# The upper part of the gated one-hot in a tile of its own, with a token's 128 elements side by side

## The chip, the cores and the metric

One core of a Trainium2 chip runs the whole program. The metric is the device time of one execution, in microseconds (us); lower is better.

## The reference

The program is a two-layer encoder trunk over 256 tokens of width 1024. Each layer is a mixer (SSD in layer 0, retention in layer 1), a PEER expert layer and a gated per-layer input; a final RMSNorm closes it. The change lies in the PEER layer alone, whose core is this:

```python
idx = jnp.take_along_axis(cand_idx, top_pos, axis=-1)   # i1 * 128 + i2, 8 heads x 16 picks a token
gate = jax.nn.softmax(top_s, axis=-1)
...
hid = jax.nn.gelu(jnp.einsum('tkd,td->tk', u[ib], xb), approximate=False)
return jnp.einsum('tk,tkd->td', (gb * hid).astype(xb.dtype), v[ib])
```

Each token picks 128 of 128 x 128 = 16384 experts (`i1` and `i2` each run over 128), takes `gelu(u . x)` for each, weights it with its gate and sums the rows of `v`.

## The kernel before

No expert is gathered. The kernel computes the inner products of all 16384 experts with all 256 tokens, and multiplies them with a gate matrix that is zero where an expert was not picked. `H` (128 partitions x 128 x 256, FP32) holds the products: partition and middle index are the two halves of the expert's number, the last index is the token.

**The loop over u** (lines 1224 to 1241) has 128 iterations a layer. An iteration loads 512 KB of `peer_u`, turns it on VectorE (L511), splits it into a rounded half `wh` on ScalarE (L516) and a rest `wl` on GpSimd (L519), and multiplies both with the normed tokens in 24 matmuls of 256 columns (L1237, L1238, L1241) into one PSUM bank `m` (two of them in turn). The next iteration takes the GELU of the bank: ScalarE writes `H` where no gate stands yet (L1201), or writes back to PSUM (L1204), and VectorE multiplies that into the gates that stand already (L1205).

**The first half of the iterations** also works off the selection (top-16, index arithmetic, softmax) on VectorE. When it is done, the second half builds the gate matrix: 64 blocks of 4 tokens, one block started in each iteration. A block passes through four iterations, one step in each, and `g_slot` issues the steps in the order mm, hot, apply, lo, each for another block:

- `g_hot`: VectorE compares an iota with the indices `i1` and `i2` of 4 tokens, which gives two one-hot planes in the FP16 tile `oh` (128 partitions x 2 x 128 x 4; the partitions are the 128 picks, the last index is the token; L1169). A second VectorE instruction multiplies the first plane with the FP16 upper part of the gates, in place (L1171). The iota and the gates (`gt`) lie in PSUM.
- `g_lo`: ScalarE multiplies the gated plane of each token with the ratio of the gate's lower to its upper part and writes it to `ol` (L1177, four instructions of 128 elements).
- `g_mm`: TensorE multiplies, for each token, the transposed second plane with the gated plane (upper part) and then with `ol` (lower part), both into the same 128 columns of a PSUM bank `g` (L1183, 8 matmuls and 8 weight loads a block). The weights `oh[:, 1, :, j]` and the moving operand `oh[:, 0, :, j]` are read with a step of 4 elements (8 bytes), `ol[:, j]` with a step of 1.
- `g_apply`: ScalarE writes the gates to `H` where the product is still to come (L1193), VectorE multiplies them into the products that stand already (L1195).

`oh` has two buffers, so `g_hot` of block b+2 waits for `g_mm` of block b, which stands just ahead of it in the same iteration. `ol` has one buffer, the PSUM banks `g` two. Behind the loop comes the sum over `v` (L1266, 12 matmuls of 512 columns for each of 128 tiles), which the change does not touch.

`diag` (L262) makes a small tile `dg` for the RMSNorms; `spread` reads it soon after. The instructions of every engine are issued in the order in which the code is written; no planner moves them.

Of the kernel before, what the change touches and what calls it, by code (L numbers as in the profile page):

```python
# [8 lines left out]
F32 = mybir.dt.float32  # L9
F32R = mybir.dt.float32r  # L10
F16 = mybir.dt.float16
I32 = mybir.dt.int32
U32 = mybir.dt.uint32
AF = mybir.ActivationFunctionType
# [4 lines left out]
P = 128  # L19
# [68 lines left out]
def trunk(ctx: ExitStack, tc: tile.TileContext, a, out, dbg=None, stop=None):  # L88
    nc = tc.nc
    pe, act, dve, pool, sp = nc.tensor, nc.scalar, nc.vector, nc.gpsimd, nc.sync  # L90
# [5 lines left out]
    small = ctx.enter_context(tc.tile_pool(name="small", bufs=2))  # L96
# [142 lines left out]
    class Sums:  # L239
# [19 lines left out]

        def diag(self, n, src=None):  # L260
            v = self.root(n, src)
            dg = small.tile([P, 2, P], F32, name="dg", tag="sq", bufs=4)  # L262
            for tb in range(2):
                dve.tensor_scalar(dg[:, tb], ident, v[:, tb:tb + 1], None, op0=OP.mult)
            return dg
# [169 lines left out]
    G1 = const.tile([P, T], F32, name="G1")  # L435
# [15 lines left out]
    ps = acc.tile([P, 512], F32, name="ps")  # L451
# [494 lines left out]
    def peer(l, st):  # L946
# [210 lines left out]
        gt = bank[2][:, :128].bitcast(F16)  # L1157
# [7 lines left out]
        def g_hot(b):  # L1165

            oh = small.tile([P, 2, P, 4], F16, name="oh", bufs=2)
            t = slice(4 * b, 4 * b + 4)
            dve.tensor_tensor(oh, i4.unsqueeze(1).to_broadcast([P, 2, P, 4]),  # L1169
                              G3[:, 0:2, t].unsqueeze(2).to_broadcast([P, 2, P, 4]), op=OP.is_equal)  # L1170
            dve.tensor_mul(oh[:, 0], oh[:, 0], gt[:, t].unsqueeze(1).to_broadcast([P, P, 4]))  # L1171
            return oh, small.tile([P, 4, P], F16, name="ol", bufs=1)

        def g_lo(b, oh, ol):
            for j in range(4):
                t = 4 * b + j
                act.activation(ol[:, j], oh[:, 0, :, j], AF.Copy, scale=G1[:, t:t + 1])  # L1177

        def g_mm(oh, ol):
            ps = gps.tile([P, 512], F32, name="g")  # L1180
            for j in range(4):
                for i in range(2):
                    pe.matmul(ps[:, j * P:(j + 1) * P], oh[:, 1, :, j], ol[:, j] if i else oh[:, 0, :, j],  # L1183
                              start=j == 0 and i == 0, stop=i == 1, skip_group_check=True)
            return ps

# [20 lines left out]
        def g_slot(i, times=lambda: None):  # L1207

            ap, mm, lo, b = gst["ap"], gst["mm"], gst["lo"], gst["next"]
            gst.update(ap=None, mm=lo, lo=None)  # L1210
            if mm:
                gst["ap"] = mm[0], g_mm(*mm[1])
            if b < T // 4 and not bg:
                gst["lo"] = b, g_hot(b)
                gst["next"] += 1
            if ap:
                g_apply(*ap, i)
            if lo:
                g_lo(lo[0], *lo[1])
            times()  # L1220
            return ap or mm or lo
# [236 lines left out]
```

## Time and profile before

| | |
|---|---|
| median of 3 runs | 2245.3 us (2243.55 to 2249.71) |
| profiled execution | 2246.1 us, its span 2244.2 us |
| TensorE (PE) busy | 2165.3 us, 96% of the span |
| weight loads (PEld) | 2006.2 us, 89% |
| VectorE (DVE) | 1563.2 us, 70% |
| ScalarE (ACT) | 1210.4 us, 54% |
| GpSimd (POOL) | 878.4 us, 39% |
| blocks of the gate matrix | 128 (64 a layer), first `g_hot` at 521.1 us, last at 1833.8 us |

The span runs from the first to the last instruction; the 1.9 us beside it are the launch. Busy times of PE come from matmuls whose ends are modelled, and a matmul's duration overlaps the next one's; what a matmul costs in a dense stretch is read from the distance of two starts. PE's weight loads run beside its matmuls. In rows, L1183 names the line, `g<-oh` is a matmul of the upper part and `g<-ol,oh` one of the lower part.

### The profile page before, as it was taken

What the parts mean: (1) busy time and instruction counts of PE and PEld (TensorE: products, weight loads), DVE (VectorE), ACT (ScalarE), POOL (GpSimd) and SP (SyncE); (2) the same over time, 40 slices, a digit from 0 to 9 for tenths busy, and PEclk for the clock granted to TensorE, in tenths of its full rate; (3) what the DMA queues carried; (4) which work ended last, traced back from release to release, by engine and by line L of the source; (5) the groups of instructions that cost most, each with busy time, mean ns of one, the idle gap of its engine ahead of it and who ended that gap; (6) DMA issues with size and microseconds to landing.
All of it is one profiled execution on the core that took longest, in us unless ns stands there. A gap on an engine that the chain in (4) does not pass through costs nothing. (4 is left out here: it accounts for less than half of the span.)

```text
span 2244.2 us, 39809 instructions
## 1 busy us (share of the span) xinstructions
PE 2165.3 (96%) x15013; PEld 2006.2 (89%) x15013; DVE 1563.2 (70%) x2625; ACT 1210.4 (54%) x2063; POOL 878.4 (39%) x408
## 2 busy tenths in 40 slices
PE   7899899999999999999989999999999999999997
PEld 7788899999999888888888999999999998888886
DVE  7478678887788655555587366889678875555556
ACT  4544444546888644444553444445588874444444
POOL 5743248886666200000044123788766640000002
PEclk9999999999999999999999999999999999999998
DMA  5432467756555555555645455776555545666653
GB/s 165 136 106 86 143 192 181 183 139 160 143 148 144 160 195 190 196 193 192 201 160 174 138 166 177 176 191 154 160 148 145 145 147 194 193 194 192 194 192 104
DMA packets 219577, 370.27 MB, mean 165 GB/s; under 512 B 24240, under 2 KB 163192, under 8 KB 219384
## 3 DMA queue, kind: packets, MB, share of 16 engines
q1 hardware_dynamic: 219064, 367.19, 55.0%
q8 instruction: 118, 1.93, 0.4%
q14 instruction: 75, 0.61, 0.1%
q10 hardware_dynamic: 320, 0.53, 0.1%
HBM read 364.48 MB, written 1.05 MB: 163 GB/s over the span
## 5 line engine op out<-in xcount | busy, mean ns | idle before, releaser
L135 ACT CAST wh<-raw 128x1024 fp32r<-128x1024 f32 x429 | 450.3, 1052 | 519.7 <-PE ps L1266 362.5
L138 DVE TENSOR_TENSOR wl<-raw,wh 128x1024 fp32r<-128x1024 f32 x365 | 453.6, 1246 | 393.9 <-ACT wh L135 393.9
L519 POOL TENSOR_TENSOR wl<-raw,wh 128x1024 fp32r<-128x1024 f32 x256 | 615.5, 2406 | 240.5 <-ACT wh L516 231.1
L1266 PE MATMUL ps<-wh,X 128*128 128x512 f32 x2048 | 509.2, 390 | 4.6 <-ACT X L186 4.6
L1237 PE MATMUL m<-X,wh 128*128 128x256 f32 x2048 | 512.9, 288 | 0.6 <-ACT arena L1201 0.6
L1238 PE MATMUL m<-X,wh 128*128 128x256 f32 x2048 | 501.8, 283 | 0.0
L1266 PEld LDWEIGHTS ps<-wh,X 128*128 128x128 f32 x2048 | 385.0, 188 | 85.3 <-ACT X L186 5.0
L516 ACT CAST wh<-raw 128x1024 fp32r<-128x1024 f32 x256 | 269.1, 1051 | 274.9 <-issue 157.1
L1237 PEld LDWEIGHTS m<-X,wh 128*128 128x128 f32 x2048 | 392.8, 192 | 1.2 <-ACT arena L1201 1.0
L1238 PEld LDWEIGHTS m<-X,wh 128*128 128x128 f32 x2048 | 391.2, 191 | 0.0
L198 PE MATMUL ps<-X,wh 128*128 128x256 f32 x2368 | 333.6, 291 | 14.7 <-ACT wh L135 8.4
L340 POOL TENSOR_TENSOR arena<-arena 128x512 f32<-128x512 f32 x15 | 22.5, 1502 | 825.2 <-ACT arena L338 824.8
L198 PEld LDWEIGHTS ps<-X,wh 128*128 128x128 f32 x2368 | 307.5, 197 | 20.7 <-ACT wh L135 10.4
L1241 PE MATMUL m<-X,wl 128*128 128x256 f32 x2048 | 287.4, 283 | 0.1
L1266 PE MATMUL ps<-wl,X 128*128 128x512 f32 x1024 | 274.7, 389 | 0.0
L1241 PEld LDWEIGHTS m<-X,wl 128*128 128x128 f32 x2048 | 264.1, 191 | 0.7 <-POOL wl L519 0.7
L1266 PEld LDWEIGHTS ps<-wl,X 128*128 128x128 f32 x1024 | 192.4, 188 | 40.1
L138 POOL TENSOR_TENSOR wl<-raw,wh 128x1024 fp32r<-128x1024 f32 x64 | 165.5, 2597 | 157.6 <-ACT wh L135 157.5
L511 DVE STREAM_TRANSPOSE raw<-raw 128x1024 f32<-128x1024 f32 x144 | 179.2, 1244 | 50.1 <-DMA raw<-in_peer_u 37.4
L198 PE MATMUL ps<-X,wl 128*128 128x256 f32 x1184 | 178.9, 289 | 15.6 <-POOL wl L138 8.0
L198 PEld LDWEIGHTS ps<-X,wl 128*128 128x128 f32 x1184 | 159.6, 196 | 18.0 <-DVE wl L138 9.0
L1177 ACT ACTIVATE ol<-oh,G 128x128 f16<-128x128 f16 x512 | 168.4, 401 | 1.5 <-PE g L1183 0.3
(263 smaller groups left out, 2158.9 us busy)
## 6 DMA issues: line engine op xcount, KB each, us to landing
raw<-in_peer_v SPq DMA_DIRECT2D x256, 512.0 KB, 4.3
raw<-in_peer_u SPq DMA_DIRECT2D x576, 128.0 KB, 3.0
arena<-in_peer_u SPq DMA_DIRECT2D x448, 128.0 KB, 3.3
raw<-in_ret_w_in SPq DMA_DIRECT2D x48, 512.0 KB, 4.1
raw<-in_ssd_w_in SPq DMA_DIRECT2D x41, 512.0 KB, 3.7
raw<-in_peer_w_q SPq DMA_DIRECT2D x32, 512.0 KB, 4.8
raw<-in_ssd_w_out SPq DMA_DIRECT2D x16, 512.0 KB, 3.6
raw<-in_ple_gate SPq DMA_DIRECT2D x16, 512.0 KB, 4.5
```

The lines of the kernel that those rows point to most:

```text
L135: act.copy(wh[:, :n], r[:, :n])
L138: (eng or dve).tensor_sub(wl[:, :n], r[:, :n], wh[:, :n].bitcast(F32))
L198: pe.matmul(self.t[n // 2][:, n % 2], w[:, n * P:(n + 1) * P], x, start=st, stop=sp_, skip_group_check=True)
L340: pool.tensor_add(self.sq[:, 0], self.sq[:, 0], self.sq[:, b])
L511: dve.transpose(t.rearrange("p (k b i) -> p b k i", k=8, b=4), r.rearrange("p (b k i) -> p b k i", k=8, b=4))
L516: act.copy(wh, t)
L519: pool.tensor_sub(wl, t, wh.bitcast(F32))
L1177: act.activation(ol[:, j], oh[:, 0, :, j], AF.Copy, scale=G1[:, t:t + 1])
L1237: pe.matmul(last, wh[:, s], xh, start=k == 0, stop=False)
L1238: pe.matmul(last, wh[:, s], xl, start=False, stop=False)
L1241: pe.matmul(last, wl[:, s], xh, start=False, stop=k == KD - 1)
L1266: pe.matmul(sums[b], h[:, tb * P:(tb + 1) * P], w[:, n * 512:(n + 1) * 512], start=i == 0 and p == 0, stop=i == P - 1 and p == 2)
```

## The change

The gated upper part is no longer written back into `oh`. A new tile `hl` (2 x 4 x 128 in FP16, name `ol`, two buffers) holds for each token the 128 elements of the upper part side by side, and behind them the lower part. The multiplication on VectorE reads the plane of `oh` with the token outermost (a step of 8 bytes from element to element), and its gate operand repeats one value along the last dimension. ScalarE reads the upper part from `hl`, and TensorE's moving operand has a step of 1 for both parts. The weights `oh[:, 1, :, j]` stay as they were. `dg` gets two buffers in place of four; each partition uses 1 KB more of SBUF in all.

```diff
-            dg = small.tile([P, 2, P], F32, name="dg", tag="sq", bufs=4)
+            dg = small.tile([P, 2, P], F32, name="dg", tag="sq", bufs=2)
...
             dve.tensor_tensor(oh, i4.unsqueeze(1).to_broadcast([P, 2, P, 4]),
                               G3[:, 0:2, t].unsqueeze(2).to_broadcast([P, 2, P, 4]), op=OP.is_equal)
-            dve.tensor_mul(oh[:, 0], oh[:, 0], gt[:, t].unsqueeze(1).to_broadcast([P, P, 4]))
-            return oh, small.tile([P, 4, P], F16, name="ol", bufs=1)
-
-        def g_lo(b, oh, ol):
+            hl = small.tile([P, 2, 4, P], F16, name="ol", bufs=2)
+            dve.tensor_mul(hl[:, 0], oh[:, 0].rearrange("p i t -> p t i"), gt[:, t].unsqueeze(2).to_broadcast([P, 4, P]))
+            return oh, hl
+
+        def g_lo(b, oh, hl):
             for j in range(4):
                 t = 4 * b + j
-                act.activation(ol[:, j], oh[:, 0, :, j], AF.Copy, scale=G1[:, t:t + 1])
-
-        def g_mm(oh, ol):
+                act.activation(hl[:, 1, j], hl[:, 0, j], AF.Copy, scale=G1[:, t:t + 1])
+
+        def g_mm(oh, hl):
             ps = gps.tile([P, 512], F32, name="g")
             for j in range(4):
                 for i in range(2):
-                    pe.matmul(ps[:, j * P:(j + 1) * P], oh[:, 1, :, j], ol[:, j] if i else oh[:, 0, :, j],
+                    pe.matmul(ps[:, j * P:(j + 1) * P], oh[:, 1, :, j], hl[:, i, j],
                               start=j == 0 and i == 0, stop=i == 1, skip_group_check=True)
```

No instruction is added, removed or moved on any engine; operands and waits change. On VectorE, one steady iteration of the loop over u stood like this (`oh` and `ol` are the tiles of a block, `ps` the PSUM banks with iota and gates, `g` a block's result, `m` the bank of products; the waits name the engines' semaphores):

```order
L511 STREAM_TRANSPOSE raw<-raw 128x4x8x32 [waits DMAHW5_49,DMAHW4_49,DMAHW6_49,DMAHW3_49,Pool_49]
L1169 TENSOR_TENSOR oh<-ps,G_98 128x1024 [waits PE_49]
L1171 TENSOR_TENSOR oh<-oh,ps 128x512 [waits DVE_49]
L1195 SCALAR_TENSOR_TENSOR arena<-g,arena 128x84x4 [waits Activation_49]
L1205 TENSOR_TENSOR arena<-arena,m 128x72
```

The same iteration of the changed kernel, whose lines are numbered one higher from the multiplication on:

```order
L511 STREAM_TRANSPOSE raw<-raw 128x4x8x32 [waits DMAHW5_49,DMAHW4_49,DMAHW6_49,DMAHW3_49,Pool_49]
L1169 TENSOR_TENSOR oh<-ps,G_98 128x1024 [waits PE_49]
L1172 TENSOR_TENSOR ol<-oh,ps 128x512 [waits DVE_49,Activation_49]
L1196 SCALAR_TENSOR_TENSOR arena<-g,arena 128x84x4 [waits Activation_49]
L1206 TENSOR_TENSOR arena<-arena,m 128x72
```

Nothing moved; the multiplication writes the other tile and has a second wait, for the `g_lo` that last used the same buffer, two blocks earlier. On ScalarE the first `g_lo` instruction of a block waited for VectorE and TensorE, and now waits for VectorE alone. On TensorE, the first half of a block before:

```order
L1183 LDWEIGHTS oh [waits DVE_49]
L1183 MATMUL g<-oh 128x128 [waits PE_49]
L1183 LDWEIGHTS oh
L1183 MATMUL g<-ol,oh 128x128 [waits Activation_49]
L1183 LDWEIGHTS oh
L1183 MATMUL g<-oh 128x128
```

And in the changed kernel:

```order
L1184 LDWEIGHTS oh [waits DVE_49]
L1184 MATMUL g<-ol,oh 128x128 [waits PE_49]
L1184 LDWEIGHTS oh
L1184 MATMUL g<-ol,oh 128x128 [waits Activation_49]
L1184 LDWEIGHTS oh
L1184 MATMUL g<-ol,oh 128x128
```

The order and the waits are the same; the upper part's matmul now reads the tile `ol` as well.

## Rows read from the trace of the kernel before

**Rows 1.** Windows in the two steady stretches: us, then busy time of each engine.

```profile
546.00:740.00 194.00, 194.00 (x1706) 191.64 (x1705) 159.35 (x266) 157.18 (x428) 127.69 (x54) 1.00 0.52 145
1634.00:1830.00 196.00, 196.00 (x1729) 193.68 (x1728) 162.43 (x270) 158.75 (x433) 129.66 (x55) 1.00 0.52 146
```

**Rows 2.** Timeline of 600 to 612 us, PE: start, length, instruction.

```profile
600.58 0.66 PEld L1183 LDWEIGHTS <-oh 128*128 128x128 f16 x8
600.59 0.29 PE L1183 MATMUL g<-oh 128*128 128x128 f16 x1
600.69 0.24 PE L1183 MATMUL g<-ol,oh 128*128 128x128 f16 x1
600.77 0.28 PE L1183 MATMUL g<-oh 128*128 128x128 f16 x1
...
600.87 0.24 PE L1183 MATMUL g<-ol,oh 128*128 128x128 f16 x1
600.94 0.28 PE L1183 MATMUL g<-oh 128*128 128x128 f16 x1
...
601.04 0.24 PE L1183 MATMUL g<-ol,oh 128*128 128x128 f16 x1
601.12 0.28 PE L1183 MATMUL g<-oh 128*128 128x128 f16 x1
...
601.22 0.24 PE L1183 MATMUL g<-ol,oh 128*128 128x128 f16 x1
...
603.15 0.28 PE L1238 MATMUL m<-X,wh 128*128 128x256 f32 x1
...
603.27 1.12 PE L1241 MATMUL m<-X,wl 128*128 128x256 f32 x8
...
604.91 0.37 PE L1237 MATMUL m<-X,wh 128*128 128x256 f32 x1
```

**Rows 3.** Groups of instructions by shape: count, busy us, mean ns of one.

```profile
L1177 ACT ACTIVATE ol<-oh,G 128x128 f16<-128x128 f16 x512 | 168.4, 401 | 1.5 <-PE g L1183 0.3
...
L1183 PE MATMUL g<-oh 128*128 128x128 f16 x512 | 104.1, 280 | 1.4 <-DVE arena L1195 0.7 <-DVE oh L1171 0.6
...
L1183 PE MATMUL g<-ol,oh 128*128 128x128 f16 x512 | 97.8, 238 | 0.3 <-ACT ol L1177 0.3
L1169 DVE TENSOR_TENSOR oh<-ps,G 128x1024 f16<-128x1024 f16 x128 | 88.1, 688 | 57.7 <-PE g L1183 57.7
...
L1171 DVE TENSOR_TENSOR oh<-oh,ps 128x512 f16<-128x512 f16 x128 | 53.8, 421 | 4.5
```

**Rows 4.** The same view, VectorE instructions of other stages.

```profile
L1068 DVE TENSOR_TENSOR arena<-arena,ps 128x1024 f16<-128x1024 f16 x16 | 19.1, 1196 | 0.1
...
L693 DVE TENSOR_TENSOR arena<-arena 128x512 f32<-128x512 f32 x4 | 6.6, 1650 | 0.0
```

**Rows 5.** Waits in 546 to 740 us: who waited for whom, us in total, times, longest.

```profile
DVE oh L1169 <- PE g L1183: 26.6, 53, 0.5
DVE raw L511 <- POOL wl L519: 5.0, 21, 0.3
```

**Rows 6.** Timeline, VectorE, one early and one late iteration; idle ahead in brackets.

```profile
602.22 0.42 DVE L1171 TENSOR_TENSOR oh<-oh,ps 128x512 f16<-128x512 f16 x1
602.56 0.51 DVE L1195 SCALAR_TENSOR_TENSOR arena<-g,arena 128x344 f32<-128x344 f32 x1
602.99 0.23 DVE L1205 TENSOR_TENSOR arena<-arena,m 128x80 f32<-128x80 f32 x1
...
740.07 0.69 DVE L1169 TENSOR_TENSOR oh<-ps,G 128x1024 f16<-128x1024 f16 x1 [0.47 <-PE g L1183]
```

**Rows 7.** Waits in 515 to 546 us, the first iterations that build the gate matrix.

```profile
PEld L1183 <- DVE arena L1195: 0.9, 2, 0.6
...
PE g L1183 <- DVE oh L1171: 0.6, 1, 0.6
PE g L1183 <- DVE arena L1195: 0.4, 1, 0.4
```

## The prediction

> **What bounds the kernel now.** I read the windows of the two steady stretches first, because the change touches only the second half of each loop over u. There PE is busy for all of the time, 194.00 of 194 us and 196.00 of 196 us, while VectorE, ScalarE and GpSimd are busy for 159, 157 and 128 us of the first [rows 1]. So TensorE sets the pace, and a nanosecond that a matmul gives up there is a nanosecond of the program, until another engine catches up. The other engines count only for how much room they leave.
>
> Second, the timeline of one block's 8 matmuls [rows 2]. A matmul's length there (0.24 to 0.29 us) is no cost, since it overlaps the next; the distance of two starts is. From an upper-part matmul to the lower-part one behind it I read 600.59 to 600.69, 600.77 to 600.87, 600.94 to 601.04, 601.12 to 601.22: 0.10 us four times. From a lower-part matmul to the next upper-part one: 0.08, 0.07, 0.08, mean 0.077. Both kinds have 128 columns in FP16 and the same weights, read in the same way; the moving operand's step is the difference one sees. The groups say it too: 280 ns for one upper-part matmul against 238 for a lower-part one, 512 of each [rows 3].
>
> **TensorE's part of the change.** After it the upper part is read as the lower part is now. Weight loads stay as they are, and they already keep step with the 0.077. So I price an upper-part matmul at the lower one's distance. 0.100 - 0.077 = 0.023; starts are printed to 0.01 us, which leaves about 0.020 to 0.025, and I take 0.022. A block has 4 of them: 0.09 us an iteration. The two layers have 512: 512 x 0.022 = 11.3 us less. Bounds: nothing, if the step isn't what makes them slow (first rival), and 512 x 0.042 = 21.5 us, if the whole difference in length counted; the weight loads' step of 0.077 speaks against that end, so I stay near the distances.
>
> [...]
>
> **VectorE's part.** The comparison (L1169) takes 688 ns for 1024 elements and the multiplication (L1171) 421 ns for 512 [rows 3]: 267 ns for 512 elements more, 0.52 ns each, and 154 ns fixed. This is two elements in the time that L1068 takes for one: also FP16 with a PSUM operand that repeats along the last dimension, 1196 ns for 1024, so (1196 - 154) / 1024 = 1.02 ns each [rows 4]. The new multiplication has a repeated PSUM operand and a stepped source, so I give it that rate: 154 + 512 x 1.02 = 0.68 us, 0.26 more than before. Bounds: 0.42 us, if nothing changes, and 1.65 us, the longest VectorE product of 512 elements in the trace (L693, other operands) [rows 4]. TensorE reads the same plane with the same 8-byte step today, 128 elements in 0.10 us [rows 2]: 0.78 ns an element, so memory hands them out faster than the one per 1.02 ns that VectorE would ask for. I stay at 0.68.
>
> Is there room for 0.26 us? VectorE idles ahead of L1169 for 26.6 us in 53 iterations, waiting for the block's matmuls, and ahead of L511 for 5.0 us, waiting for GpSimd [rows 5]: together 0.60 us an iteration. An instruction that need not wait starts 0.08 us before the end of the one ahead (602.22 + 0.42 = 602.64, next start 602.56) [rows 6], so without the waits some 0.1 us more is gained: about 0.70 us of room at the old pace, 0.61 at the new one. In a late iteration (740 us) L511 waits no more and the room is 0.47 + 0.08 - 0.09 = 0.46 us [rows 6]. 0.26 fits in both; the waits shrink to some 0.15 to 0.3 us, and the cost is nothing. What stands behind the multiplication on VectorE comes 0.26 us later: L1195, L1205 and L511. PE waits for L1205 two banks on: it ended at 603.22 and the next L1237 started at 604.91 [rows 2, 6], 1.7 us of slack. If the room were gone, each 0.1 us too much would cost 0.1 us in each iteration, some 11 us over the 110 steady ones.
>
> **Where the cover is missing.** In the first iterations of a layer's gate matrix VectorE still works off the selection, and PE waits for it: 0.6 us for the first multiplication, 0.4 and 0.9 us for L1195 [rows 7], four waits in the first layer. Each has at least one multiplication ahead of it on VectorE. I add 0.26 us to four waits, for both layers together, since VectorE's own waits for data there may take part of it: 1.1 us more. Bounds: nothing, and 0.26 us for four waits in each layer, 2.1.
>
> **Parts that cost nothing.** ScalarE's four instructions read a step of 1 in place of 8 bytes. It is busy 157 of 194 us, so neither a gain nor a loss of some ns shows. Its wait for TensorE ended with matmuls that had just been issued ahead of VectorE's, and cost it 0.3 us in the whole program [rows 3], so nothing comes back. VectorE's new wait for ScalarE is for a `g_lo` that the block's matmuls, for which the comparison ahead waits anyway, had to await too. With two `dg` buffers a third norm would wait; each `dg` is read by `spread` before the next but one is made, and the issue order has at most one open. The loads get 0.09 us less for 512 KB; the stretch moves 145 GB/s with the DMA engines busy 0.52 of the time [rows 1], so they have the room.
>
> **The sum.** -11.3 + 1.1 = -10.2 us. The profiled execution took 2246.1 us (span 2244.2 and 1.9 around it), 0.8 above the median of 2245.3. 2246.1 - 10.2 = 2235.9; I give 2236, which is 0.4% below either.
>
> **Rivals.** 0.3%, 6.7 us, is about what a measurement can tell from no change here.
>
> First: the change doesn't do what it says, because the step isn't the cause. Two other things differ between the two kinds of matmul. The lower-part one waits for a semaphore of ScalarE each time, long since given, and it adds into the columns that the upper-part one has just begun to write; either could hold its start by 0.02 us, and both stay. Against the first: the first L1241 waits for GpSimd and starts 0.12 us after L1238, and the eight of them take 1.12 us, that is 0.12 a step, wait or no wait [rows 2]. Against the second: those also add into one bank's columns again and again. Against both: the upper-part matmul itself is 42 ns longer. Then only the 1.1 us remain: 2247 us. Chance 0.12. [...]
>
> [...] Chance 0.12.
>
> Third, on the other side: VectorE becomes the bound. That happens when the multiplication grows by more than the 0.70 us of room at the old pace, from 1.12 us on. If it took 2.1 ns an element, four times today's 0.52, it would be 154 + 1075 = 1.23 us, 0.81 more, and 110 iterations would each be 0.11 us longer than before: +12 us, with the start +3: 2261 us. For it speaks L693 with 1.65 us, against it that L693 has two SBUF sources while GpSimd works, and L1171 has kept 421 ns beside a GpSimd that is busy for two thirds of the stretch. Chance 0.06.
>
> **How the numbers follow.** The forecast has 0.70. From 2236 its own range reaches from 2232 (a distance of 0.025 us, no cost at the start, spread of the runs) to 2239. The second rival brings the range to 2243; the first and third, 0.18, stay outside. Faster by over 0.3% (below 2238.6): the forecast and a slice of the second rival, 0.72. Within 0.3%: the first rival and most of the second, 0.21. Slower: 0.07.
>
> **What would show it.** In the new profile the distance of starts in a block should be 0.08 throughout and all matmuls of L1184 some 238 ns; the multiplication (L1172) about 680 ns in all 128; the iteration in steady state 0.09 us shorter (194 us hold 53 of them now); VectorE's wait ahead of L1169 about half of what it is, but still there; PE busy throughout both stretches. It is wrong if upper-part matmuls stay at 0.10 us from start to start, or if VectorE no longer waits for PE late in the loop and PE shows waits for L1172, L1196 or L1206.

## The result

The changed kernel takes 2214.14 us (median of 4 runs, 2209.17 to 2217.73) against 2246.37 for the one before (4 runs): ratio 0.9857, 95% interval 0.9835 to 0.9878. That is 32 us less (27 to 37 by the interval), three times the 10 us that I had forecast. In a second set of runs, on the chip of the last two experiments, it was 2216.31 against 2245.95, ratio 0.9874 (0.9852 to 0.9896). The profiled execution took 2216.94 us with a span of 2215.2, 29.0 less than the span before. In the experiments below a ratio can differ by up to 0.2% from the quotient of the two medians; its interval goes with the ratio.

First the windows of the steady stretches, as in [rows 1]:

```profile
546.00:740.00 194.00, 194.00 (x1825) 191.55 (x1823) 180.72 (x282) 159.91 (x456) 134.84 (x56) 1.00 0.55 158
1620.00:1800.00 180.00, 180.00 (x1693) 177.58 (x1692) 170.42 (x265) 149.31 (x424) 127.47 (x53) 1.00 0.56 156
```

TensorE still sets the pace, but in the same 194 us it now gets 1825 matmuls done in place of 1706. VectorE's busy time rose from 159 to 181 us, because more iterations fit in and each has the longer multiplication.

The groups, which answer to [rows 3]:

```profile
L1178 ACT ACTIVATE ol<-ol,G 128x128 f16<-128x128 f16 x512 | 162.8, 397 | 0.1
...
L1172 DVE TENSOR_TENSOR ol<-oh,ps 128x512 f16<-128x512 f16 x128 | 88.0, 688 | 13.2
L1169 DVE TENSOR_TENSOR oh<-ps,G 128x1024 f16<-128x1024 f16 x128 | 87.0, 679 | 3.1 <-PE g L1184 1.5
L1184 PE MATMUL g<-ol,oh 128*128 128x128 f16 x1024 | 82.5, 222 | 2.3 <-DVE arena L1196 2.0
```

The multiplication takes 688 ns, as priced. ScalarE's instruction is unchanged (397 against 401 ns). The matmuls come to 222 ns, not to the 238 that the lower-part ones had: these became shorter too, though nothing in their own operands changed. And VectorE's wait ahead of L1169 went from 57.7 to 1.5 us.

The timeline of one block on TensorE, which answers to [rows 2]; eight matmuls without a break stand in one row:

```profile
600.11 0.64 PE L1184 MATMUL g<-ol,oh 128*128 128x128 f16 x8
...
600.56 0.36 PE L1238 MATMUL m<-X,wh 128*128 128x256 f32 x1
...
600.76 0.28 PE L1239 MATMUL m<-X,wh 128*128 128x256 f32 x1
```

From the first start to the last end a block takes 0.64 us; before it was 600.59 to 601.22 + 0.24 = 601.46, 0.87 us [rows 2]. A matmul of 0.22 to 0.25 us at the end taken off, seven steps share about 0.40 us: 0.056 to 0.06 each. So 0.23 us a block, 128 blocks, 29.4 us: the whole gain of the profiled execution. The matmul ends are modelled, but starts alone say the same: to the second product behind the block it was 0.88 us (600.59 to 601.47) and is now 0.65 (600.11 to 600.76). The row of the kernel before:

```profile
601.47 0.28 PE L1238 MATMUL m<-X,wh 128*128 128x256 f32 x1
```

### The profile page after: what moved, and what is told of

Read it like the earlier page. It is cut to its first block, busy times and chain, and to the rows that moved or that the text cites. A ratio compares the mean times of both kernels' runs of the same rounds, so it can differ in the third digit from the quotient of the medians.

```text
span 2215.2 us, 39807 instructions
## 1 busy us (share of the span) xinstructions
PE 2135.2 (96%) x15013; PEld 1976.3 (89%) x15013; DVE 1587.6 (72%) x2625; ACT 1196.1 (54%) x2063; POOL 878.9 (40%) x408
## 5 line engine op out<-in xcount | busy, mean ns | idle before, releaser
L1238 PE MATMUL m<-X,wh 128*128 128x256 f32 x2048 | 512.6, 288 | 0.0
L1239 PE MATMUL m<-X,wh 128*128 128x256 f32 x2048 | 502.0, 283 | 0.0
L1239 PEld LDWEIGHTS m<-X,wh 128*128 128x128 f32 x2048 | 393.0, 192 | 0.0
L1238 PEld LDWEIGHTS m<-X,wh 128*128 128x128 f32 x2048 | 392.2, 192 | 0.3
L511 DVE STREAM_TRANSPOSE raw<-arena 128x1024 f32<-128x1024 f32 x112 | 138.4, 1237 | 43.9 <-POOL wl L519 29.0
```

The costliest lines, as they stand in the source:

```text
L511: dve.transpose(t.rearrange("p (k b i) -> p b k i", k=8, b=4), r.rearrange("p (b k i) -> p b k i", k=8, b=4))
L1238: pe.matmul(last, wh[:, s], xh, start=k == 0, stop=False)
L1239: pe.matmul(last, wh[:, s], xl, start=False, stop=False)
```

## The experiments

Some experiments read other elements than the changed kernel, so they compute something else in the same instructions; each text says which elements. Times stand beside the kernel before, run on the same chip. As a measure from the rows I use the distance from a block's first matmul to the second product behind it (L1239; L1238 in the numbering of the kernel before), since the first product behind a block lies partly under the block's last matmul (above it starts at 600.56, the block ends at 600.75): 0.65 us in the changed kernel.

### Only TensorE's step put back, and the step in both parts

```diff
-                    pe.matmul(ps[:, j * P:(j + 1) * P], oh[:, 1, :, j], hl[:, i, j],
+                    pe.matmul(ps[:, j * P:(j + 1) * P], oh[:, 1, :, j], hl[:, i, j] if i else hl[:, 0].rearrange("p t i -> p (t i)").rearrange("p (i s) -> p i s", s=4)[:, :, j],
```

> The changed kernel, but TensorE reads the upper part from the new tile with a step of 4 elements again (it then multiplies elements of other tokens; VectorE and ScalarE do exactly what they do in the changed kernel). Theory A, all of the gain is TensorE's step, by ends 116 ns for an upper-part matmul against 56: a block takes 0.24 us more, 128 blocks 31 us, so about 2245 us, as before the change (up to 2248 with the slower product on VectorE). Rival, the gain came from elsewhere (the second buffer of ol, ScalarE's lost wait, the reads of ScalarE): the time stays within 5 us of the changed kernel's 2214.

Measured: 2245.77 us against 2244.91, ratio 1.0007 (0.9995 to 1.0018). The step alone takes the whole gain back; the tile, the second buffer, ScalarE's lost wait and the slower multiplication together make 0.9 us of difference (by the interval from 1 us less to 4 us more). The block on TensorE is the old one, 0.87 us long, 0.88 us to the second product:

```profile
621.78 0.87 PE L1184 MATMUL g<-ol,oh 128*128 128x128 f16 x8
622.46 0.37 PE L1238 MATMUL m<-X,wh 128*128 128x256 f32 x1
622.66 0.28 PE L1239 MATMUL m<-X,wh 128*128 128x256 f32 x1
```

Next, the same for both parts (`hl[:, i]` in place of `hl[:, 0]` for every matmul):

> As the run before, with both parts read at a step of 4 elements (the products are then of other tokens' elements). Theory A, a stepped read costs 60 ns in each matmul that makes it: 8 x 60 ns more per block than in the changed kernel, 128 blocks, 61 us, about 2275 us. Theory B, it is the change of step from one matmul to the next that costs: nothing changes from matmul to matmul here, so about 2214 to 2220 us.

Measured: 2265.88 us, ratio 1.0110 (1.0087 to 1.0132). Theory B (the change of step from one matmul to the next) falls: here nothing changes, and the block is the longest so far.

```profile
621.99 1.11 PE L1184 MATMUL g<-ol,oh 128*128 128x128 f16 x8
622.86 0.37 PE L1238 MATMUL m<-X,wh 128*128 128x256 f32 x1
623.06 0.28 PE L1239 MATMUL m<-X,wh 128*128 128x256 f32 x1
```

All eight matmuls are alike now (296 ns long in the groups), so one length taken off the block and the rest shared by seven gives the pace of one kind alone: (1.11 - 0.30) / 7 = 0.116 us. Against 0.056 that is 0.060 for each stepped matmul. The time rose by 20 us over the run before (23 by the ratios), not by the 31 that 4 x 0.060 x 128 gives, and stayed below the 2275 us that I had expected. The rows show where the rest went: the second product comes 1.07 us behind the block's first matmul, 0.19 more than the 0.88 above and not 0.24. The first product behind the block has a hold of its own there (the next one starts 0.20 us behind it, where the others stand 0.12 apart), and I take it that a part of the stepped matmul now lies under that; no run tests it. 0.19 x 128 = 24 us.

### The weights' step

Here the weights are read side by side, so they are one-hots of other tokens; first in the changed kernel, then in the kernel before (where the upper part keeps its step).

```diff
-oh[:, 1, :, j]
+oh[:, 1, j * 32:(j + 1) * 32].rearrange("p i t -> p (i t)")
```

> The changed kernel, with the weights read at a step of 1 too (128 elements side by side of the same tile, so the rows of other tokens' one-hots). Theory A: matmuls of 56 ns are already at the pace of their 128 columns, the loads keep up, so no change: 2214 us within 5. Rival, the stepped weight loads still hold the block (as I took the 77 ns for their pace in the prediction): the starts come closer than 56 ns and some us are gained, at most 128 x 8 x 10 ns = 10 us.

Measured: 2215.21 us, ratio 0.9887 (0.9866 to 0.9907), the changed kernel's time within the spread. The weight load itself became shorter, 97 ns against 115, and the block 0.62 us against 0.64, 2.6 us over 128 blocks, which the times don't resolve:

```profile
L1184 PE MATMUL g<-ol,oh 128*128 128x128 f16 x1024 | 79.6, 221 | 3.3 <-DVE arena L1196 3.3
L1184 PEld LDWEIGHTS <-oh 128*128 128x128 f16 x1024 | 57.3, 97 | 9.1 <-DVE arena L1196 3.7
```

> The kernel before the change, with the weights read at a step of 1 (other tokens' one-hots) and the upper part still at a step of 4. Theory A, the moving operand's step alone costs: still 116 ns by ends, 2246 us as before within 5. Theory C, it costs only because weights and moving operand are both read with a step at the same time: about 56 ns, and 2215 us.

Measured: 2239.45 us against 2244.91, ratio 0.9984 (0.9971 to 0.9996): some 4 us of the 32, by the medians 5.5, and slightly more than the 5 that I had allowed. Theory C (both operands stepped at a time) falls; the moving operand's step costs by itself. The rows show the alternation of [rows 2] once more:

```profile
622.50 0.27 PE L1183 MATMUL g<-oh 128*128 128x128 f16 x1
622.60 0.24 PE L1183 MATMUL g<-ol,oh 128*128 128x128 f16 x1
622.67 0.28 PE L1183 MATMUL g<-oh 128*128 128x128 f16 x1
622.77 0.24 PE L1183 MATMUL g<-ol,oh 128*128 128x128 f16 x1
622.85 0.28 PE L1183 MATMUL g<-oh 128*128 128x128 f16 x1
```

0.10 from upper to lower, 0.07 to 0.08 from lower to upper, with weights that now load faster (a median of 98 ns in place of 115). So the 0.077 was not the pace of the weight loads.

### The size of the step

```diff
-hl[:, 0].rearrange("p t i -> p (t i)").rearrange("p (i s) -> p i s", s=4)[:, :, j]
+hl[:, 0].rearrange("p t i -> p (t i)").rearrange("p (i s) -> p i s", s=2)[:, j // 2 * P:j // 2 * P + P, j % 2]
```

and, for 16 bytes, the same over the whole tile with `s=8`. The minus line is that of the first experiment.

> The changed kernel, with the upper part read at a step of 2 elements, 4 bytes (elements of other tokens). Theory S1, any step other than 1 costs the same, some 0.9 ns an element: 116 ns by ends and 2245 us. [...]

Measured: 2218.18 us against 2243.12, ratio 0.9886 (0.9869 to 0.9902). A step of 4 bytes costs nothing that shows, 0.65 us to the second product as in the changed kernel. That excludes theory S1. Theory S2, that the cost goes with the bytes passed over, allows it: 128 x 4 bytes are as many as 128 columns of 4-byte elements, and L1238 of the kernel before stands at 0.12 us for 256 of those [rows 2], 0.47 ns each, from which I estimate 0.060 us.

```profile
622.75 0.64 PE L1184 MATMUL g<-ol,oh 128*128 128x128 f16 x8
...
623.40 0.28 PE L1239 MATMUL m<-X,wh 128*128 128x256 f32 x1
```

> The changed kernel, with the upper part read at a step of 8 elements, 16 bytes, over the whole tile (elements of other tokens and of both parts). Theory S1: 116 ns by ends, 2245 us. Theory S2, by bytes: twice the 116 ns, some 230 ns, (230 - 56) x 512 = 89 us more than the changed kernel, 2303 us.

Measured: 2296.00 us, ratio 1.0233 (1.0216 to 1.0251). The forecast of theory S2 was 2303. A step of 16 bytes adds nearly three times what one of 8 does:

```profile
623.64 1.31 PE L1184 MATMUL g<-ol,oh 128*128 128x128 f16 x8
...
624.96 0.28 PE L1239 MATMUL m<-X,wh 128*128 128x256 f32 x1
```

To the second product it is 1.32 us, 0.67 more than in the changed kernel; over four stepped matmuls 0.168 each, on top of 0.056 some 0.22 us. For 8 bytes the same sum is (0.88 - 0.65) / 4 = 0.058, some 0.115. So 0.9 ns an element at 8 bytes and 1.75 at 16: twice the step, twice the time (theory S2). At 4 bytes I estimate by the same proportion 0.45 ns an element, 0.057 us for 128, which is no more than a matmul without a step takes (0.056), and nothing shows.

### How near VectorE is to the bound

The changed kernel ran again in these runs, for comparison:

> The changed kernel once more, to stand beside the next two on one chip: 2214 us within 4.

Measured: 2216.31 us against 2245.95. Beside it the multiplication in its old, quick form (the new tile then holds the elements in the wrong order):

```diff
-dve.tensor_mul(hl[:, 0], oh[:, 0].rearrange("p i t -> p t i"), gt[:, t].unsqueeze(2).to_broadcast([P, 4, P]))
+dve.tensor_mul(hl[:, 0].rearrange("p t i -> p (t i)").rearrange("p (i s) -> p i s", s=4), oh[:, 0],
+               gt[:, t].unsqueeze(1).to_broadcast([P, P, 4]))
```

> The changed kernel, but the multiplication on VectorE keeps the order of the plane (both operands and the result with the token innermost, as before the change), so the new tile holds the right elements in the wrong order. It should take 420 ns in place of 687. Theory A, TensorE is the bound and VectorE just fits: only the waits of the first iterations shrink, 0 to 4 us less than the changed kernel, 2211 to 2214. Rival, VectorE has become a bound beside TensorE at the new pace (its wait for the block's matmuls is almost gone): 0.1 us in many iterations, 8 to 15 us less, below 2207.

Measured: 2217.59 us, ratio 0.9881 (0.9860 to 0.9902) to the kernel before, no better than the changed kernel. The multiplication took 422 ns, and VectorE was busy for 169 us of the stretch in place of 181, TensorE for all of it as before:

```profile
546.00:740.00 194.00, 194.00 (x1824) 191.52 (x1823) 169.12 (x283) 160.07 (x456) 134.54 (x56) 1.00 0.56 158
```

So the longer multiplication costs nothing that these times resolve; the 1.1 us that I had charged for the start of the gate matrix is too little to tell from them. Then the multiplication issued twice (the second writes the same values):

> The changed kernel with the multiplication issued twice (same result), 0.69 us more on VectorE in each block: the mechanism of my third rival, with a size that I know. In the changed kernel VectorE is idle for 13.3 us of 194 us, 57 iterations, 0.23 us each, with the overlap of starts about 0.28. Theory A: VectorE then sets the pace, 0.69 - 0.28 = 0.41 us in some 114 iterations, 47 us more, about 2261 us (2250 to 2275). Rival, VectorE's waits elsewhere hide it: below 2235 us.

Measured: 2279.68 us, ratio 1.0148 (1.0127 to 1.0169), 63 us more than the changed kernel and above the range that I had given. VectorE sets the pace: TensorE, which waited for nothing in the stretch from 546 to 740 us, now waits in nearly every iteration of it.

```profile
PEld L1185 <- DVE arena L1197: 26.1, 50, 0.7
PE g L1185 <- DVE arena L1197: 15.6, 46, 0.5
```

63 / 128 = 0.49 us a block. The second multiplication starts 0.72 us behind the first (601.45 and 602.17), so the room was 0.72 - 0.49 = 0.23 us in the mean, not the 0.28 that I had read from the first stretch. What I overlooked is that the room shrinks along the loop. From block to block L1196 and L1206 handle more elements (0.51 and 0.23 us at 602 us, 0.67 and 0.39 at 732). With the doubled multiplication, where VectorE sets the pace, two starts of L1169 stand 3.81 us apart (600.69 and 604.50). Less the 0.72 that is 3.09 us for VectorE's own work in the changed kernel, beside 3.41 for an iteration (eleven blocks start from 600.11 to 634.18 us): 0.32 us of room there, and none at the end of the loop. There VectorE goes in the changed kernel from block to block without a wait, in 3.41 us:

```profile
1798.58 0.65 DVE L1169 TENSOR_TENSOR oh<-ps,G 128x1024 f16<-128x1024 f16 x1
...
1801.99 0.65 DVE L1169 TENSOR_TENSOR oh<-ps,G 128x1024 f16<-128x1024 f16 x1
```

## Why the prediction was wrong

**The step that failed** is the price of a matmul of the upper part: "I price an upper-part matmul at the lower one's distance", 0.022 us gained on each. The mechanism was right, the step of the moving operand on TensorE holds the upper-part matmul, and putting that step back alone undid the whole gain. The term of the sum was mis-sized: -11.3 us, where the rows of the block give -29.4 in the profiled execution. By the distance of starts a pair took 0.10 + 0.077 = 0.177 us and now takes 2 x 0.056 = 0.112: 0.065 a pair, not 0.022. The seven distances of a block are three and a half pairs, which gives the 0.23 us.

**What I misread.** In an alternating row I took each distance of starts for the cost of one matmul, as the part ahead of the prediction says of dense stretches in general. With the costs that the experiments gave, 0.116 and 0.056, some 0.02 us of the stepped matmul's cost did not stand in the distance behind its own start (0.10) but in the 0.077 ahead of it, which I then gave to the lower-part matmul as its fair price. The ends in [rows 2], start plus length, tell it apart: 600.88, 600.93, 601.05, 601.11, 601.22, 601.28. An upper-part matmul ends 0.11 to 0.12 us after the one ahead, a lower-part one 0.05 to 0.06. Those are, to the 0.01 us of the print, the 0.116 and 0.056 of the rows with eight matmuls of one kind. The ends are modelled, but the sum of the pair was not in doubt, and nothing in the trace showed that a lower-part matmul alone needs 0.077. A row that the prediction itself read spoke against it: the eight L1241 stand 0.12 us apart with 256 columns (of another type), and half of that, as an estimate for 128 columns, is 0.06.

**The false support** was "weight loads ... already keep step with the 0.077". With the same stepped weights matmuls now follow each other at 0.056, and weights without a step brought no gain that shows in the changed kernel and 4 to 5.5 us in the one before. The bound that I named for the gain, 512 x 0.042 = 21.5 us, was the difference in length and no bound either: lengths overlap.

**The other steps.** The new multiplication was priced at 0.68 us and took 0.688; with the 154 ns that I had estimated as fixed that is (688 - 154) / 512 = 1.04 ns an element. The price came from L1068, whose PSUM operand is FP32 and repeats over a middle dimension, not along the last as I had written; so the agreement of 1.02 and 1.04 does not show one cause. The second rival, by which the range reaches 2243, puts the stepped read on VectorE higher than that; no run shows such a price, all 128 multiplications took 0.686 to 0.690 us. On TensorE's moving operand the step did cost: a matmul with a step of 8 bytes took 0.116 us in place of 0.056 with 4. My first rival, that the step isn't the cause, is excluded by the first experiment, in which the step alone brought the time back to 2245.77 us.

"VectorE's wait about half of what it is" was wrong, 1.5 of 57.7 us stayed, as a consequence of the size: with the iteration 0.23 us shorter in place of 0.09, the room of 0.70 us, less 0.23 and less 0.27, leaves 0.20, near the mean of 0.23 that the doubled multiplication found; and my late iteration leaves 0.47 + 0.08 - 0.23 - 0.27 = 0.05 in place of some 0.2. Half of a sign that I had named for being wrong came true: late in the loop VectorE no longer waits for PE, but for the last `g_hot` of each layer (two waits, 1.5 us in all). The other half did not, PE shows no such waits there but one of 0.2 us, of a weight load, behind 1740 us. The change came closer to the third rival than I knew, without paying for it.

The 1.1 us for the first iterations was not seen. In 515 to 546 us TensorE's matmuls waited for VectorE for 0.6 + 0.4 us before [rows 7] and for 1.1 us after, now for L1196, which reads out an earlier block:

```profile
PE g L1184 <- DVE arena L1196: 1.1, 1, 1.1
```

The parts that I had priced at nothing showed nothing: ScalarE and the `dg` buffers by the first experiment, within its interval, and the loads by the windows, where TensorE stays busy throughout while the traffic rises from 145 to 158 GB/s.

What stays open: why the stamp of a stepped matmul's start comes early, and why the first product behind a block is held. Both were only read from rows, not tried. On VectorE the stepped read and the gate operand that repeats along the last dimension came together, so it is not shown which of them makes 1.04 ns an element out of 0.52.

## What to carry to other kernels

Give TensorE's moving operand elements that lie close together, and let an engine with room pay for the reordering; here 0.27 us on VectorE bought 0.23 us on TensorE in each iteration, and only TensorE's counted, down to the last iterations of each layer, where VectorE's room was used up. Where matmuls of two kinds alternate, take the cost from the sum over a whole pair and split it by ends, or look for a stretch of one kind; a single distance of starts can belong to the neighbour. And before a large gain is booked on the bounding engine, count the room of the next one at the new pace, where it is smallest: it was 0.23 us of 3.4 in the mean and nothing at the end of the loop.

## What the runs showed of the hardware

- A moving operand of 128 FP16 columns took 0.056 us a matmul with a step of 2 or 4 bytes, 0.116 with 8 and some 0.22 with 16: at 8 and 16 bytes the time goes with the bytes passed over, about 0.11 ns each. Larger steps and other types were not run.
- The weights' step of 8 bytes made a load of 128 columns 115 ns in place of 97 in the changed kernel; of these 8 x 18 = 144 ns a block the block's length shows 0.02 us (0.64 in place of 0.62).
- VectorE read 512 FP16 elements at a step of 8 bytes, beside an FP16 operand in PSUM that repeats along the last dimension, in 688 ns; L1068, with an FP32 operand in PSUM that repeats over a middle dimension and no step, takes 1196 ns for 1024 [rows 4]. With 154 ns as fixed, an estimate from L1169 and L1171 [rows 3], that is 1.04 and 1.02 ns an element. ScalarE needed 401 ns with the step and 397 without.
